# Hybrid decoder layer in fp32 on one core: the first FFN pass's norm and half of its operands made during the mixers, the sample states loaded ahead, an output projection placed later

## The chip, the core and the metric

The kernel runs on one core of a Trainium2 chip. Work is shared by TensorE (PE in the profile; PEld is its weight load), VectorE (DVE), ScalarE (ACT), GpSimd (POOL) and SyncE (SP), which here issues every DMA from one queue, in order. Each engine executes its own list of instructions in the order in which it was written. The metric is the time of one execution on the device in microseconds (us).

## The reference

One layer over 2048 prompt tokens and 8 x 4 sample tokens, width 1024. Two head groups run in parallel (the mixers): HGRN2, a gated linear recurrence with 4 heads, and a causal convolution of width 31 over 512 channels. Then comes a SwiGLU feed-forward network (FFN), a per-layer embedding behind a gate, and a last norm.

```python
xn = _rmsnorm(h, norm_mix)
proj = xn @ w_in                      # q, fg, iv, og, ca, cg
forget = lb + (1.0 - lb) * sigmoid(fg)
o, s_new = _hgrn2_scan(silu(q), 1.0 - forget, iv, log(forget), s0)
o_a = _rmsnorm(o, hgrn_out_norm) * silu(og)
u = ca * sigmoid(cg)
z = depthwise_conv(concat(buf0, u)) + conv_dw_bias
o_b = silu(layer_norm(z))
h = h + concat(o_a, o_b) @ w_out
xn2 = _rmsnorm(h, norm_ffn)
h = h + (silu(xn2 @ w_ffn_gate) * (xn2 @ w_ffn_up)) @ w_ffn_down
gate = sigmoid(_rmsnorm(h, norm_ple) @ w_ple_gate)
h = h + gate * (p_l @ w_ple_proj)
y = _rmsnorm(h, norm_final)
```

The sample tokens start from given states s0 (8 states of 128x128 for each head); the new states are outputs too.

## The kernel before

**Precision.** Every large product is made of three matmuls in fp32r: each operand is split into a high part (ACT copies it, tiles wh, xah, xoh, x2h) and a low part (DVE subtracts, tiles wl, xal, xol, x2l; `split` and `split_piece`, recorded at L368 and L373).

**Mixers.** The tokens are 8 blocks of 256 (the last has the 32 sample tokens as well), two blocks to a superblock, so superblocks 0 to 3. For each superblock PE makes 24 units of input projection (ca, cg, iv, f, q, og) from the normed operand XA and 8 units of output projection ("o") from XO. Superblocks 1 and 2 do both blocks in one matmul of 512 columns; 0 and 3 do them as two lanes of 256 (or 288) columns. The list `seq` sets the order of the units: after the units of superblock s, the first `AFTER` = 12 input units of s + 1, then the 8 output units of s, then the other input units of s + 1. Between them run the convolution (31 DVE taps for each channel group, L376), the recurrence (`hgrn`, 4 heads one after another for each block, one at a time) and, when all 4 channel groups of a block are there, the layer norm over channels (`layer_norm`, PE transposes L921 and L953). In the last block `hgrn` also takes the sample states: for each head 4 times it gets a tile of pool `tmp`, loads two states into it (t<-s_in), uses and updates them on PE (L1136, L1145) and DVE, and stores them. Pool `tmp` has 8 tiles, which the convolution and others use too.

**FFN.** When all that is recorded, the memory of the mixers is given over to the FFN's tiles (`open_scope("ffn")`), the event "ffn" is fired, and only then are the output units of superblock 3 recorded, on PE ahead of the FFN. The FFN goes over the tokens in 3 passes of two halves (348 tokens). Gate and up are a Strassen-like product with 7 combinations (A11, A12, S1, ...) of 4 quarter operands. For pass t `norm2(t)` loads the residual stream h1 back from DRAM, makes the row factors r2 of both halves (`rms2`: ACT squares, DVE sums, PE transposes L1618, DVE reductions L1613 to L1625, POOL power L409, PE transposes L1633), and `combine(t, kp, ...)` for kp = 0 to 3 loads and scales four pieces and splits the 7 combinations into slots X2. The slots of kp 0 and 1 lie in the memory of XA, those of kp 2 and 3 (x2h, x2l) in the FFN's memory. Pass 0 needs blocks 0 to 2 only.

The 22 hidden tiles go in chunks of 4, 4, 4, 4, 4, 2 (`CHUNKS`). After a chunk's gate and up (`gate_up`, L1354) comes the down product of the chunk before it (`down`), and at the end of a pass the down products of the last two chunks one after the other, then the gated embedding (`embed`). With the last down product each finished piece of h2 is split into an operand of the embedding (`h2_split`), which takes a slot of pool `hid` (16 slots; a hidden tile takes one for each half until its chunk's down product is done).

**Order.** A planner with fixed costs records each engine's instructions: of the steps that are ready it takes the one that could start first, and between steps of an engine that could start at nearly the same time the one with the lower number (the second argument of `spawn`; convolution 400 and 700, recurrence 0 and 250, weight splits 10, `combine` 0). Pools hand out buffers in the order of the requests.

Of the kernel before, what the change touches and what calls it, by code (L numbers as in the profile page):

```python
# [8 lines left out]
F32R = mybir.dt.float32r  # L9
# [23 lines left out]
CHUNKS = (4, 4, 4, 4, 4, 2)  # L33
# [22 lines left out]
AFTER = 12  # L56
# [179 lines left out]
def trunk(ctx: ExitStack, tc: tile.TileContext, x_in, p_in, s0_in, c0_in, w_in, w_out, w_gu, w_dn,  # L236
# [52 lines left out]


# [331 lines left out]
    def lane(L):  # L622
        for i, (s, u, lanes) in enumerate(seq):
# [362 lines left out]
    def hgrn(b, L, h, f):  # L986
# [130 lines left out]
        if samp:  # L1117
# [10 lines left out]
                     [scss, vs], [bo])  # L1128
            for g in range(4):
                s0 = yield acq(tmp)  # L1130
                s3 = s0.ap[:, 0:256].rearrange("p (b v) -> p b v", b=2)
                yield dma(s3, s0_in[h, :, 2 * g:2 * g + 2, :], W=[s0], nbytes=512 * 256)
# [16 lines left out]
                yield tt(s0.ap[:, 0:256], s0.ap[:, 0:256], b2.ap[:, 0:256], ALU.add, R=[s0, b2], W=[s0], n=256)  # L1149
# [3 lines left out]
                S.release(tmp, s0)  # L1153
# [41 lines left out]
        if done[b] == HEADS:  # L1195
            if samp:
                S.release(hg, *ivs.pop(b))
            S.fire(("hgdone", b))

# [17 lines left out]
    S.spawn(lane(1), 30)  # L1217
    manual = tc.manual_schedule()
# [8 lines left out]
    def cut(tiles, count):  # L1227

        return [tuple(Buf(t[:, i * WID:(i + 1) * WID]) for t in tiles) for i in range(count)]

    def flat(i, count):
        f = hbuf[i].rearrange("p k t -> p (k t)")
        return [Buf(f[:, j * WID:(j + 1) * WID]) for j in range(count)]

    xslots = cut(za, 16) + cut([tm("x2" + p, [128, 12 * WID], F32R) for p in "hl"], 12)
    X2 = [{name: xslots[kp * len(COMBOS) + i] for i, name in enumerate(COMBOS)} for kp in range(KP)]
# [7 lines left out]

    PASSES = range(len(HALF))
    HALVES = range(2)
    last_chunk = NCK - 1
# [304 lines left out]
    def segs(t, h):  # L1552

        lo, out = OFF[t] + h * HALF[t], []
        for b in range(NBLK):
            x, y = max(lo, b * BLK), min(lo + HALF[t], b * BLK + blk_n(b))
            if x < y:
                out.append((b, x - b * BLK, x - lo, y - x))
        return out

    def h1_load(t, h, k, q):
        n, lo = HALF[t], OFF[t] + h * HALF[t]
        for b, _, _, _ in segs(t, h):
            yield wait(("h1", b, k // 2))
        yield dma(q.ap[:, 0:n], h1d[:, k, lo:lo + n], W=[q], nbytes=512 * n)

    res, n3, pins = {}, {}, {}

    def residual():
        for t in PASSES:  # L1570
            for m in range(KD):
                for h in HALVES:
                    q = yield acq(hres)
                    yield from h1_load(t, h, m, q)
                    res[t, m, h] = q
                    S.fire(("hr", t, m, h))

    def free_h(b, idx, count):
        for i in range(KD // 2):
            yield wait(("h1", b, i))  # L1580
        S.release(hres, *flat(idx, count))

    def squares2(n, get, sq, tag):
        for k in range(KD):
            src, q = yield from get(k)
            yield act(q.ap[:, 0:n], src.ap[:, 0:n], AF.Square, scale=D ** -0.5, R=[src], W=[q], n=n)
            sq[k] = q
            S.fire(("sq", tag, k))

    def rms2(n, get):  # L1590

        tk = toks(n)
        tag, sq = count[0], {}
        count[0] += 1
        S.spawn(squares2(n, get, sq, tag), PSQ)
        acc = [None, None]
        for i in range(KD):
            yield wait(("sq", tag, i))
            if i < 2:
                acc[i] = sq[i]  # L1600
                continue
            a, q = acc[i % 2], sq[i]
            if i == 2:
                yield stt(a.ap[:, 0:n], a.ap[:, 0:n], EPS / 128, q.ap[:, 0:n], ALU.add, ALU.add, R=[a, q], W=[a], n=n)
            else:
                yield tt(a.ap[:, 0:n], a.ap[:, 0:n], q.ap[:, 0:n], ALU.add, R=[a, q], W=[a], n=n)
            S.release(tmp2, q)
        a, q = acc
        yield tt(a.ap[:, 0:n], a.ap[:, 0:n], q.ap[:, 0:n], ALU.add, R=[a, q], W=[a], n=n)
        S.release(tmp2, q)  # L1610
        ss = yield acq(small)
        tn = tk[-1][1]
        yield op("dve", 80.0, lambda: nc.vector.memset(ss.ap[:, 2:3], 1.0), [], [ss])  # L1613
        bank = yield acq(misc)

        def fn():
# [235 lines left out]
```

## Time and profile before

| | us |
|---|---|
| median of 3 runs | 2723.65 (2722.88 to 2724.57) |
| the profiled execution | 2725.04 |
| its span in the trace | 2723.3 |
| PE busy | 2566.1 (94%) |
| DVE busy | 1999.1 (73%) |
| ACT busy | 1071.4 (39%) |

The profiled execution took 1.7 us more than its span and lies 1.4 us over the median. PE carries nearly all of the span, so what can be read from the table is little; the question is where PE stood still or ran at a lower clock, and for what.

### The profile page before, as it was taken

How to read it: one execution, taken by the hardware profiler on the slowest of the kernel's cores; microseconds unless marked ns; L12 is line 12 of the kernel's file. 1: busy time of each engine (PE TensorE's matmuls, PEld its weight loads, DVE VectorE, ACT ScalarE, POOL GpSimd, SP SyncE). 2: the span in 40 equal slices, each digit the busy share in tenths (PEclk: the TensorE clock that was granted, in tenths of full speed). 3: DMA queues.
4: the chain of work that ended last, by engine and by line, in shares of the span. 5: the costliest groups of instructions: out<-in, count | busy, mean ns of one | idle time of the engine just before them, and what ended most of it. 6: DMA issues, size and time to landing. Idle time of an engine off the chain costs nothing.

```text
span 2723.3 us, 43381 instructions
## 1 busy us (share of the span) xinstructions
PE 2566.1 (94%) x15886; PEld 2409.8 (88%) x15886; DVE 1999.1 (73%) x4506; ACT 1071.4 (39%) x2397; POOL 134.1 (5%) x286
## 2 busy tenths in 40 slices
PE   7999899999998659999999899999998999999996
PEld 6988777778787559999999899999998999999996
DVE  8999888888768557666668686766677776666664
ACT  5553233333113225344444443544345444433441
POOL 0111011021001000000000000000000000000000
PEclk9999899999998679999999899999999999999998
DMA  8656555654555262232213133322232252212311
GB/s 307 219 189 220 179 173 197 207 171 147 183 175 168 94 196 74 71 116 78 82 62 111 66 118 115 123 78 71 70 113 65 81 158 82 75 66 77 101 47 50
DMA packets 219078, 338.66 MB, mean 124 GB/s; under 512 B 38640, under 2 KB 82160, under 8 KB 218864
## 3 DMA queue, kind: packets, MB, share of 16 engines
q1 hardware_dynamic: 218864, 335.89, 37.4%
q8 instruction: 124, 2.03, 0.3%
q14 instruction: 90, 0.74, 0.1%
HBM read 282.29 MB, written 53.51 MB: 123 GB/s over the span
## 4 chain that ended last, share of the span: by engine, by line
PE 89%; DVE 6%; DMA 2%; POOL 1%; ACT 1%; issue 1%; SPq 0%; DVEq 0%; POOLq 0%; ACTq 0%
PE pm L1354 20%; PE pm L525 14%; PE pm L527 13%; PE pm L526 13%; PE px L1354 12%; PE px L525 3%; PE px L527 3%; PE px L526 3%; DVE h L373 1%; PE pm L593 1%; PE pm L595 1%; PE pm L594 1%; DVE h L376 1%; DMA t<-s_in 1%; PE px L1113 1%; PE px L1080 1%
## 5 line engine op out<-in xcount | busy, mean ns | idle before, releaser
L373 DVE TENSOR_TENSOR wl<-raw,wh 128x512 fp32r<-128x512 f32 x520 | 356.4, 689 | 200.0 <-ACT wh L368 197.1
L368 ACT ACTIVATE wh<-raw 128x512 fp32r<-128x512 f32 x520 | 323.2, 627 | 380.7 <-PE pm L526 208.2
L527 PE MATMUL pm<-xoh,wl 128*128 128x348 f32 (+4 forms) x1072 | 350.0, 326 | 14.1 <-DVE wl L373 14.1
L525 PE MATMUL pm<-xol,wh 128*128 128x348 f32 (+4 forms) x1072 | 353.7, 330 | 1.9 <-DVE xol L373 1.6
L526 PE MATMUL pm<-xoh,wh 128*128 128x348 f32 (+4 forms) x1072 | 349.6, 326 | 0.0
L525 PE MATMUL pm<-xal,wh 128*128 128x256 f32 (+2 forms) x960 | 321.0, 334 | 5.9 <-DVE xal L373 3.5
L526 PE MATMUL pm<-xah,wh 128*128 128x256 f32 (+2 forms) x960 | 309.8, 323 | 0.0
L527 PE MATMUL pm<-xah,wl 128*128 128x256 f32 (+2 forms) x960 | 309.3, 322 | 0.0
L1354 PE MATMUL pm<-xal,wh 128*128 128x348 f32 (+1 forms) x661 | 213.6, 323 | 18.0 <-DVE xal L373 14.9
L373 DVE TENSOR_TENSOR h<-pm,h 128x348 f32<-128x348 f32 (+1 forms) x263 | 135.2, 516 | 122.9 <-PE pm L527 109.8
L527 PEld LDWEIGHTS pm<-xoh,wl 128*128 128x128 f32 x1072 | 205.5, 192 | 20.3 <-DVE wl L373 14.7
L368 ACT ACTIVATE wh<-tw 128x512 fp32r<-128x512 f32 x198 | 124.8, 630 | 244.2 <-DVE tw L373 120.5
L525 PEld LDWEIGHTS pm<-xol,wh 128*128 128x128 f32 x1072 | 205.7, 192 | 12.1 <-issue 3.8
L1354 PE MATMUL pm<-xah,wh 128*128 128x348 f32 (+1 forms) x661 | 212.6, 322 | 0.0
L1354 PE MATMUL pm<-xah,wl 128*128 128x348 f32 (+1 forms) x661 | 212.4, 321 | 0.0
L376 DVE SCALAR_TENSOR_TENSOR t<-u,cvw,t 128x256 f32<-128x256 f32 x448 | 212.1, 473 | 0.0
L526 PEld LDWEIGHTS pm<-xoh,wh 128*128 128x128 f32 x1072 | 205.5, 192 | 4.5
L525 PEld LDWEIGHTS pm<-xal,wh 128*128 128x128 f32 x960 | 182.1, 190 | 29.8 <-issue 6.5
L527 PEld LDWEIGHTS pm<-xah,wl 128*128 128x128 f32 x960 | 181.4, 189 | 13.9
L526 PEld LDWEIGHTS pm<-xah,wh 128*128 128x128 f32 x960 | 182.1, 190 | 12.1
L376 DVE SCALAR_TENSOR_TENSOR h<-u,cvw,h 128x256 f32<-128x256 f32 x360 | 170.3, 473 | 0.0
L409 POOL TENSOR_TENSOR sm<-sm,mhalf 128x2 f32<-128x2 f32 (+3 forms) x79 | 67.6, 855 | 1878.2 <-DVE sm L1613 824.3
(267 smaller groups left out, 6225.9 us busy)
## 6 DMA issues: line engine op xcount, KB each, us to landing
raw<-w_gu SPq DMA_DIRECT2D x264, 256.0 KB, 2.8
wh<-wch SPq DMA_DIRECT2D x192, 256.0 KB, 2.7
wl<-wcl SPq DMA_DIRECT2D x192, 256.0 KB, 3.1
raw<-w_dn SPq DMA_DIRECT2D x132, 256.0 KB, 2.8
wch<-wh SPq DMA_DIRECT2D x64, 256.0 KB, 2.6
wcl<-wl SPq DMA_DIRECT2D x64, 256.0 KB, 3.1
raw<-w_in SPq DMA_DIRECT2D x48, 256.0 KB, 3.8
raw<-w_pg SPq DMA_DIRECT2D x48, 256.0 KB, 2.8
```

Of the source, the lines that this page charges most:

```text
L368: nc.scalar.activation(out, in_, func, scale=scale, bias=bias, **kw)
L373: return op("dve", d_tt(n), lambda: nc.vector.tensor_tensor(out=out, in0=a, in1=b, op=o), R, W)
L376: return op("dve", d_tt(n, not isinstance(s, float)), lambda: nc.vector.scalar_tensor_tensor(out=out, in0=a, scalar=s, in1=b, op0=o0, op1= ...
L409: return op("pool", 700.0, lambda: nc.gpsimd.tensor_tensor(out=s.ap[0:rows, out:out + n], in0=s.ap[0:rows, lo:lo + n], in1=mhalf[0:rows, 0 ...
L525: nc.tensor.matmul(out, lhsT=wh, rhs=xl, start=first, stop=False)
L526: nc.tensor.matmul(out, lhsT=wh, rhs=xh, start=False, stop=False)
L527: nc.tensor.matmul(out, lhsT=wl, rhs=xh, start=False, stop=last)
L593: nc.tensor.matmul(bank.ap, lhsT=xs[0], rhs=wl, start=(k == 0), stop=False)
L594: nc.tensor.matmul(bank.ap, lhsT=xs[0], rhs=wh, start=False, stop=False)
L595: nc.tensor.matmul(bank.ap, lhsT=xs[1], rhs=wh, start=False, stop=(k == KD - 1))
L1080: nc.tensor.matmul(bu[e].ap[:, c], lhsT=kt.ap[p, c], rhs=V[i].ap[p, hc], start=True, stop=True)
L1354: nc.tensor.matmul(out, lhsT=a, rhs=b, start=first and i == 0, stop=last and i == 2, skip_group_check=True)
```

## The change

1. `AFTER` becomes (12, 12, 20, 0): the output units of superblock 2 come after 20 instead of 12 input units of superblock 3. The later superblocks take their input units in the order that superblock 0 had (ca and cg of the first group ahead of iv).
2. The sample states are loaded by a step of their own, `load_states`, two tiles of 128x512 of pool `raws` for a head (4 states each), from the end of superblock 2's input units on. Pool `raws` (6 tiles) holds weights during superblock 0 and in the FFN and is empty between.
3. `norm2(0)` and `combine(0, 0)`, `combine(0, 1)` are recorded with the mixers, with number 350, as soon as tiles are free: pool `tmp2` gets its 5 tiles in `hbuf[1]` when block 5's h1 is stored (`free_tmp2`), r2 gets memory of its own, and the combinations wait until superblock 3's input units are done with XA. kp 2 and 3 wait for "ffn".
4. `CHUNKS` becomes (4, 4, 4, 4, 2, 4), and `combine` of passes 1 and 2 gets number 150 instead of 0.

The functions `segs` to `combine` are moved ahead of the mixers' spawns with no other change than the lines shown.

```diff
-CHUNKS = (4, 4, 4, 4, 4, 2)
+CHUNKS = (4, 4, 4, 4, 2, 4)
...
-AFTER = 12
+AFTER = (12, 12, 20, 0)
...
+    r2 = [Buf(tl(f"r2{h}", [128, WID])) for h in range(2)]
...
+    tmp2 = S.pool("tmp2", [])
...
-        todo = list(in_units) if s + 1 < NSUP else []
-        add(s + 1, todo[:AFTER], then)
+        todo = list(first_units) if s + 1 < NSUP else []
+        add(s + 1, todo[:AFTER[s]], then)
         add(s, outs, who if s else AB)
-        add(s + 1, todo[AFTER:], then)
+        add(s + 1, todo[AFTER[s]:], then)
...
-                if u == in_units[-1]:
+                if u == first_units[-1]:
                     S.fire(("indone", b))
...
+            yield wait(("s0", h))
+            two = stash.pop(("s0", h))
             for g in range(4):
-                s0 = yield acq(tmp)
-                s3 = s0.ap[:, 0:256].rearrange("p (b v) -> p b v", b=2)
-                yield dma(s3, s0_in[h, :, 2 * g:2 * g + 2, :], W=[s0], nbytes=512 * 256)
+                s0 = two[g // 2]
+                sa = s0.ap[:, g % 2 * 256:g % 2 * 256 + 256]
+                s3 = sa.rearrange("p (b v) -> p b v", b=2)
...
-                S.release(tmp, s0)
+            S.release(raws, *two)
...
+    def load_states():
+        yield wait(("indone", NBLK - 4))
+        for h in range(HEADS):
+            two = yield acq(raws, 2)
+            for g, s0 in enumerate(two):
+                yield dma(s0.ap.rearrange("p (b v) -> p b v", b=4), s0_in[h, :, 4 * g:4 * g + 4, :], W=[s0],
+                          nbytes=512 * 512)
+            stash["s0", h] = two
+            S.fire(("s0", h))
+
+    def free_tmp2():
+        for i in range(KD // 2):
+            yield wait(("h1", NBLK - 3, i))
+        S.release(tmp2, *flat(1, 5))
...
+    xslots = cut(za, 16)
+    X2 = [{name: xslots[kp * len(COMBOS) + i] for i, name in enumerate(COMBOS)} for kp in range(2)]
...
     def norm2(t):
...
         if t:
             yield wait(("a", t - 1, last_chunk, CHUNKS[-1] - 1, 1))
+        else:
+            yield wait(("indone", NBLK - 2))
+            yield wait(("indone", NBLK - 1))
         for kp in range(KP):
+            if t == 0 and kp == 2:
+                yield wait("ffn")
             five = yield acq(tmp2, 5)
-            S.spawn(combine(t, kp, five), 0)
+            S.spawn(combine(t, kp, five), 350 if t == 0 and kp < 2 else 150 if t else 0)
...
+    S.spawn(load_states(), 0)
+    S.spawn(free_tmp2(), 0)
+    S.spawn(norm2(0), 350)
...
-    tmp2 = S.pool("tmp2", [Buf(tm(f"f{i}", [128, WID])) for i in range(NTMP2)] + flat(1, 5))
+    S.release(tmp2, *[Buf(tm(f"f{i}", [128, WID])) for i in range(NTMP2)])
-    r2 = [Buf(tm(f"r2{h}", [128, WID])) for h in range(2)]
...
     for t in PASSES:
-        S.spawn(norm2(t), 100 if t else 0)
+        if t:
+            S.spawn(norm2(t), 100)
```

Three places show how the instructions move. **PE, from the last output unit of superblock 3 to the first gate product of the FFN** (px and pm are PSUM banks, f and h here tiles of the norm, sm its row sums; L1354 is the FFN's matmul). Before:

```order
L527 MATMUL px_177<-xoh,wl_91 128x288
L1618 MATMUL px_178<-idn,f_9007 128x128 x2
L1618 MATMUL px_178<-idn,f_9007 92x128
L1633 MATMUL px_176<-idn,sm_68 128x128 x2
L1633 MATMUL px_176<-idn,sm_68 128x92
L1618 MATMUL px_178<-idn,h_77 128x128 x2
L1618 MATMUL px_178<-idn,h_77 92x128
L1633 MATMUL px_176<-idn,sm_70 128x128 x2
L1633 MATMUL px_176<-idn,sm_70 128x92
L1354 MATMUL pm_173<-xal,wh_92 128x348
```

Of the change (L537 is the old L527, L1528 the old L1354):

```order
L535 MATMUL pm_174<-xol,wh_90 128x288
L536 MATMUL pm_174<-xoh,wh_90 128x288
L537 MATMUL pm_174<-xoh,wl_91 128x288
L1528 MATMUL pm_175<-xal,wh_92 128x348
L1528 MATMUL pm_175<-xah,wh_92 128x348
```

The four transposes of `norm2(0)` no longer stand between the output units and the FFN.

**PE, from the last input unit of superblock 3 to its first output unit** of the change (L1148 and L1157 are the sample states' matmuls, the old L1136 and L1145; L931 and L963 the layer norm's transposes; L1304 and L1319 those of `norm2(0)`):

```order
L537 MATMUL pm_173<-xah,wl_95 128x288
L1148 MATMUL px_180<-raw_103,t_152 32x128 x2
L1319 MATMUL px_178<-idn,sm_74 128x128 x2
L1319 MATMUL px_178<-idn,sm_74 128x92
L1157 MATMUL px_177<-t_155,t_148 128x256
L1148 MATMUL px_180<-raw_103,t_152 32x128 x2
L1157 MATMUL px_177<-t_154,t_148 128x256
L1194 MATMUL px_179<-idn,t_153 128x128 x2
L1196 MATMUL px_179<-idn,t_151 128x32
L1304 MATMUL px_178<-idn,h_77 128x128 x2
L1304 MATMUL px_178<-idn,h_77 92x128
L931 MATMUL px_177<-idn,h_78 128x128 x4
```

Before, six of the sixteen sample-state steps and the whole recurrence of two heads stood here; now two steps do, and one head's last transposes.

**DVE, the end of the last down product of pass 0** (h<-pm,h adds a down result to the residual, xol<-h,gn,xoh is `h2_split`, x2l and xal are combinations for pass 1). Before:

```order
L373 TENSOR_TENSOR h_78<-pm_174,h_78 128x348
L373 TENSOR_TENSOR h_78<-px_177,h_78 128x348
L373 TENSOR_TENSOR x2l<-f_9011,x2h 128x348
L376 SCALAR_TENSOR_TENSOR xol<-h_78,gn,xoh 128x348 x2
L373 TENSOR_TENSOR x2l<-f_9008,x2h 128x348
```

Of the change:

```order
L383 TENSOR_TENSOR h_78<-pm_174,h_78 128x348
L386 SCALAR_TENSOR_TENSOR xol<-h_79,gn,xoh 128x348
L386 SCALAR_TENSOR_TENSOR xol<-h_78,gn,xoh 128x348 x3
L386 SCALAR_TENSOR_TENSOR xol<-h_79,gn,xoh 128x348
L386 SCALAR_TENSOR_TENSOR xol<-h_78,gn,xoh 128x348 x3
L383 TENSOR_TENSOR wl_87<-raw_100,wh_86 128x512
L383 TENSOR_TENSOR xal<-f_9123,xah 128x348
```

Eight of the sixteen operand splits now follow the last add, and most combinations for pass 1 follow those.

## Rows read from the trace of the kernel before

**Rows 1.** The page: busy time of engines, and the span in 40 slices.

```profile
PE 2566.1 (94%) x15886; PEld 2409.8 (88%) x15886; DVE 1999.1 (73%) x4506; ACT 1071.4 (39%) x2397; POOL 134.1 (5%) x286
...
PE   7999899999998659999999899999998999999996
...
PEclk9999899999998679999999899999999999999998
```

**Rows 2.** Windows, mixers to FFN: length; busy (count) of each engine; PEclk, DMA share, GB/s.

```profile
core 0: us, PE busy (x) PEld busy (x) DVE busy (x) ACT busy (x) POOL busy (x), PEclk, DMA share, GB/s
100.00:300.00 200.00, 188.91 (x1293) 164.85 (x1292) 185.99 (x502) 87.29 (x252) 26.54 (x64) 0.98 0.55 186
633.00:867.50 234.50, 232.20 (x1538) 201.51 (x1537) 175.96 (x526) 55.25 (x163) 22.87 (x61) 1.00 0.56 174
633.00:922.30 289.30, 261.43 (x1638) 217.66 (x1636) 218.39 (x683) 65.63 (x201) 27.47 (x76) 0.91 0.49 154
750.00:800.00 50.00, 49.50 (x347) 44.45 (x346) 27.48 (x82) 9.14 (x27) 3.62 (x13) 1.00 0.58 180
867.50:934.10 66.60, 36.21 (x129) 20.55 (x127) 49.05 (x172) 13.52 (x47) 8.12 (x23) 0.55 0.18 59
934.10:985.50 51.40, 50.63 (x385) 50.40 (x384) 17.07 (x35) 9.41 (x20) 0.00 (x0) 0.96 0.71 236
985.50:1025.00 39.50, 6.90 (x22) 4.20 (x22) 29.18 (x66) 15.94 (x35) 1.71 (x2) 0.56 0.51 156
1025.00:1050.00 25.00, 24.57 (x135) 24.08 (x136) 18.87 (x37) 13.66 (x29) 0.00 (x0) 0.88 0.16 53
```

**Rows 3.** Waits of PE, 860 to 1030 us: us in total, times, longest.

```profile
PE px L1136 <- DMA t<-s_in: 22.4, 6, 4.4
PE pm L1354 <- DVE xal L373: 14.9, 3, 8.6
PE px L1618 <- DVE sm L1613: 11.7, 2, 7.6
```

**Rows 4.** Timeline of PE, the last layer norm: start, length, idle before and releaser.

```profile
922.27 2.82 PE L921 MATMUL px<-idn,h 128*128 128x128 f32 x12
...
934.05 0.58 PE L525 MATMUL pm<-xol,wh 128*128 128x256 f32 x1
```

**Rows 5.** Windows of the three ends of pass, columns as in group 2.

```profile
1490.00:1500.00 10.00, 5.88 (x34) 5.05 (x32) 10.00 (x23) 5.81 (x13) 0.00 (x0) 0.92 0.25 71
1500.00:1510.00 10.00, 3.62 (x11) 3.18 (x12) 10.00 (x22) 7.39 (x17) 0.00 (x0) 0.50 0.22 68
1510.00:1520.00 10.00, 8.41 (x48) 7.88 (x46) 9.12 (x24) 6.37 (x15) 0.97 (x1) 0.90 0.29 90
1520.00:1530.00 10.00, 9.50 (x59) 9.09 (x60) 4.94 (x11) 3.43 (x7) 1.76 (x2) 1.00 0.09 28
2050.00:2060.00 10.00, 9.12 (x57) 8.63 (x56) 10.00 (x23) 5.93 (x13) 0.00 (x0) 1.00 0.03 8
2060.00:2070.00 10.00, 1.80 (x10) 1.25 (x9) 10.00 (x23) 6.22 (x14) 0.00 (x0) 0.75 0.22 64
2070.00:2080.00 10.00, 9.32 (x45) 9.32 (x46) 10.00 (x24) 7.81 (x19) 0.00 (x0) 0.74 0.33 105
2080.00:2090.00 10.00, 8.27 (x56) 7.94 (x55) 5.39 (x16) 2.76 (x8) 3.01 (x1) 1.00 0.08 29
2600.00:2620.00 20.00, 14.62 (x92) 14.33 (x91) 19.40 (x44) 14.62 (x33) 0.00 (x0) 0.95 0.04 14
2620.00:2640.00 20.00, 20.00 (x118) 19.86 (x118) 10.46 (x25) 6.36 (x13) 2.00 (x2) 0.88 0.24 79
```

**Rows 6.** Timeline of DVE in the first of them.

```profile
1499.29 0.51 DVE L373 TENSOR_TENSOR h<-pm,h 128x348 f32<-128x348 f32 x1
1499.72 0.51 DVE L373 TENSOR_TENSOR h<-px,h 128x348 f32<-128x348 f32 x1
1500.15 0.51 DVE L373 TENSOR_TENSOR x2l<-f,x2h 128x348 fp32r<-128x348 f32 x1
1500.58 1.06 DVE L376 SCALAR_TENSOR_TENSOR xol<-h,gn,xoh 128x348 fp32r<-128x348 f32 x2
1501.56 0.51 DVE L373 TENSOR_TENSOR x2l<-h,x2h 128x348 fp32r<-128x348 f32 x1
...
1508.66 1.28 DVE L373 TENSOR_TENSOR wl<-raw,wh 128x512 fp32r<-128x512 f32 x2
1509.86 0.51 DVE L376 SCALAR_TENSOR_TENSOR f<-f,h 128x348 f32<-128x348 f32 x1
```

**Rows 7.** Timeline of PE there: down matmuls at full clock, then the longest wait.

```profile
1495.35 0.32 PE L525 MATMUL px<-xol,wh 128*128 128x348 f32 x1
1495.51 0.33 PE L526 MATMUL px<-xoh,wh 128*128 128x348 f32 x1
...
1506.31 0.66 PE L525 MATMUL pm<-hxl,wh 128*128 128x348 f32 x1 [10.32 <-ACT wh L368]
```

**Rows 8.** Waits of the SP queue, 850 to 1030 us, and one weight load, 860 to 935.

```profile
SPq L454 <- DVE h L373: 22.1, 9, 5.6
...
wl<-wcl SPq DMA_DIRECT2D x5, 256.0 KB, 5.7
```

More of the change, by code (lines that the diff above doesn't have):

```diff
@@ L288, in trunk, with flat @@
     wcache = [dram.tile([64, 128, 512], F32, name="wc" + p) for p in "hl"]
+    r2 = [Buf(tl(f"r2{h}", [128, WID])) for h in range(2)]
+    def flat(i, count):
+        f = hbuf[i].rearrange("p k t -> p (k t)")
+        return [Buf(f[:, j * WID:(j + 1) * WID]) for j in range(count)]
+    tmp2 = S.pool("tmp2", [])
     open_scope("mix")
@@ new lines, in cut, with segs @@
+    def cut(tiles, count):
+        return [tuple(Buf(t[:, i * WID:(i + 1) * WID]) for t in tiles) for i in range(count)]
+    PASSES = range(len(HALF))
+    HALVES = range(2)
+    last_chunk = NCK - 1
+    xslots = cut(za, 16)
+    X2 = [{name: xslots[kp * len(COMBOS) + i] for i, name in enumerate(COMBOS)} for kp in range(2)]
+    def segs(t, h):
+        lo, out = OFF[t] + h * HALF[t], []
+        for b in range(NBLK):
+            x, y = max(lo, b * BLK), min(lo + HALF[t], b * BLK + blk_n(b))
+            if x < y:
+                out.append((b, x - b * BLK, x - lo, y - x))
+        return out
@@ new lines, in h1_load, with residual @@
+    def h1_load(t, h, k, q):
+        n, lo = HALF[t], OFF[t] + h * HALF[t]
+        for b, _, _, _ in segs(t, h):
+            yield wait(("h1", b, k // 2))
+        yield dma(q.ap[:, 0:n], h1d[:, k, lo:lo + n], W=[q], nbytes=512 * n)
+    res, n3, pins = {}, {}, {}
+    def residual():
+        for t in PASSES:
+            for m in range(KD):
+                for h in HALVES:
+                    q = yield acq(hres)
+                    yield from h1_load(t, h, m, q)
+                    res[t, m, h] = q
+                    S.fire(("hr", t, m, h))
@@ new lines, in row, with norm2, get @@
+    def row(n, get, r, ev):
+        bank = yield from rms2(n, get)
+        yield act(r.ap[:, 0:n], bank.ap[:, 0:n], AF.Copy, R=[bank], W=[r], n=n)
+        S.release(misc, bank)
+        S.fire(ev)
+    def norm2(t):
+        if t:
+            yield wait(("a", t - 1, 2, 0, 1))
+        for h in HALVES:
+            def get(k, h=h):
+                q = yield acq(tmp2)
+                yield from h1_load(t, h, k, q)
+                return q, q
+            yield from row(HALF[t], get, r2[h], ("r2", t, h))
+        if t:
+            yield wait(("a", t - 1, last_chunk, CHUNKS[-1] - 1, 1))
+        else:
+            yield wait(("indone", NBLK - 2))
+            yield wait(("indone", NBLK - 1))
+        for kp in range(KP):
+            if t == 0 and kp == 2:
+                yield wait("ffn")
+            five = yield acq(tmp2, 5)
+            S.spawn(combine(t, kp, five), 350 if t == 0 and kp < 2 else 150 if t else 0)
@@ L1567, in trunk @@
[L1567 to L1588, printed above, removed]
@@ L1639, in row @@
-    def row(n, get, r, ev):
-        bank = yield from rms2(n, get)
-        yield act(r.ap[:, 0:n], bank.ap[:, 0:n], AF.Copy, R=[bank], W=[r], n=n)
-        S.release(misc, bank)
-        S.fire(ev)
-    def norm2(t):
-        if t:
-            yield wait(("a", t - 1, 2, 0, 1))
-        for h in HALVES:
-            def get(k, h=h):
-                q = yield acq(tmp2)
-                yield from h1_load(t, h, k, q)
-                return q, q
-            yield from row(HALF[t], get, r2[h], ("r2", t, h))
-        if t:
-            yield wait(("a", t - 1, last_chunk, CHUNKS[-1] - 1, 1))
-        for kp in range(KP):
-            five = yield acq(tmp2, 5)
-            S.spawn(combine(t, kp, five), 0)
```

176 lines of the change are left out of this document (83 added, 93 removed).

## The prediction

> **What bounds the kernel now.** First the page: PE is busy 94% of the span, DVE 73%, and in the 40 slices PE dips at the mixers' end (8, 6, 5) and slightly at three later places; the granted clock dips in the same slices [rows 1]. So the kernel is bound by PE except there, and a change can only gain where PE stands still or runs at the lower of its two clock levels (1.2 instead of 2.4 GHz, a granted clock of 0.50). I therefore cut the dips into windows.
>
> At the end of the mixers [rows 2] PE is full until 867.5 us, when superblock 3's input units end. From 867.5 to 934.1 it is busy 36.21 of 66.6 us at a granted clock of 0.55: these are the small matmuls of the recurrence, waiting for DVE, ACT and, for 22.4 us in six pieces, for the sample states' loads [rows 3]. From 934.1 to 985.5 it makes the output units, full. From 985.5 to 1025 it is busy 6.90 of 39.5 us at 0.56: `norm2(0)` and the first combinations, DVE work on which PE waits (L1618 11.7 us, xal 14.9 us) [rows 3]. At 1025 the gate product runs for good.
>
> Behind that, each pass has a hole at the last down product [rows 5]. There DVE is busy 10.00 of 10 us, and PE waits 10.32 us for a weight whose split is queued behind other work [rows 6, 7]. The output projection's and FFN's other stretches are full, and nothing is to be had there.
>
> **The change part by part.** The sum is made against the profiled execution's 2725.04 us, 1.4 us over the median 2723.65; the difference goes through unchanged.
>
> *Mixers to FFN (parts 1 to 3).* What PE does from 867.5 to 1025 is, counted at full clock, 36.21 x 0.55 + 50.63 x 0.96 + 6.90 x 0.56 = 19.9 + 48.6 + 3.9 = 72.4 us of 157.5 [rows 2]. With every wait gone the gate product could start at 867.5 + 72.4 = 939.9, 85.1 us sooner, and the 24.57 us behind 1025 at 0.88 would save another 2.9: a ceiling of 88.0 us. The parts share it and can't be added singly: state loads alone are in it with at most 22.4.
>
> Can DVE follow? The operands of superblock 3 are split at 633, and from there to the layer norm of the last block (922.3) DVE is busy 218.4 of 289.3 us, 75% [rows 2]. Its idle 71 us lie mostly before 867.5 (234.5 - 176.0 = 58.5), the worst stretch being 750 to 800 at 55%, when PE works on the output units of superblock 2 and hands DVE little. Those units now come 8 input units later, so DVE gets superblock 3's convolutions and heads earlier. To its 218.4 us the change adds the sums of `norm2(0)`: 14 adds, 0.43 us apart [rows 6], and four reductions of about 0.35, 7.4 us together. So 226 us; at the 93% that DVE reaches from 100 to 300 [rows 2] that is 243 us, and the layer norm can start at 876. PE has 867.5 plus what it no longer does in the tail: of the 19.9 us some 16 now lie among the projections, so it arrives at about 884. PE is the later one, by 8 us.
>
> From the layer norm to the first output unit took 11.8 us (922.27 to 934.05) [rows 4], about 3.4 us of it PE work at full clock (6.8 at half), so 8.4 are kept. The output units kept 0.96 of the clock; I keep their 2.0 us too. I give 2 to 3 more for DVE being late here and there. That leaves 85.1 + 2.9 - 8.4 - 2.0 - 2.6 = **75 us**.
>
> The moved work must be hidden: a combination group is 4 scalings 0.49 us apart (1.06 for two in [rows 6]) and 11 adds or splits of 0.43, 6.7 us of DVE, four groups 26.8. Two are written ahead of the output units and two beside them. Beside the 51.4 us of output units DVE was busy only 17.07 [rows 2]; there now fall 13.4 us of kp 2 and 3, perhaps 13 of kp 0 and 1 if late, 16 adds of about 0.4 (6.4) and 11 weight splits or differences of 0.60 (6.6): 39 of 51.4. If that cover were gone, the old stall of 39.5 us would be back.
>
> Loads: the states are 8 loads of 256 KB instead of 16 of 128 KB, issued around 633, before superblock 3's first head has its operands, and hidden there; the fourth head's tiles come from the first's. The 32 loads of h1 for `norm2(0)` and `combine(0)` move on the SP queue ahead of weights of superblock 3's output units. SP already stands waiting for DVE to free tiles (22.1 us in nine waits) [rows 8]. A wait there holds the weights behind it, but four of the eight output units have theirs loaded before, 25 us of PE work. The Trainium skill, "DMA: Bandwidth & Descriptors", Anatomy of one DMA, says that a DMA's semaphore wait is taken on the issuing sequencer before dispatch, so everything behind it on that queue is late too; by that rule the moved loads could give back part of the gain, which is a rival below. The rows on SP agree that the queue waits, but show no PE wait on wch or wcl in that stretch.
>
> The new order of units at a superblock's start (ca and cg before iv): superblock 3's ca needs all 8 operand pieces in 2.6 us of PE where iv took longer, so PE may wait a little for splits; against it convolutions start earlier. Between 0 and +3 us per superblock; I take 0 and leave 5 in the range.
>
> *Ends of pass (part 4).* The holes [rows 5], idle time plus busy time x (1 - granted clock): pass 0, 4.1 + 6.4 + 1.6 + 0.5 idle and 3.1 of clock, 15.7; pass 1, 0.9 + 8.2 + 0.7 + 1.7 and 2.9, 14.4; pass 2, 5.4 and 3.1, 8.5. Together 38.6 us. Cause: with a last chunk of 2, PE takes 6 matmuls of 0.16 us [rows 7] for a piece of h2, 0.96 us, and DVE owes for each an add 0.43, an operand split 0.49, a sum for the norm 0.43 and weights 0.15: 1.5 us. With a chunk of 4 PE takes 1.92, DVE 1.65, and combinations, which had come ahead of weight splits, now come after. The chunk of 2 stands one down product earlier, where DVE owes only the add and weights, 0.6 against 0.96.
>
> What it costs: the last chunk now holds 8 of the 16 slots of `hid` until its last matmul, so eight operand splits fall behind it. The embedding uses the first four k of half 0 in 1.9 us, then wants one each 0.48 us while a pair of splits takes about 1: 1 to 2 us of waiting a pass. PE's waits for the norm's transposes stay (about 1.8 in passes 0 and 1). Kept: 9 of 38.6, gain **30 us** (ends: 0, if the late splits cost what the hole did, and 38.6).
>
> Sum: 75 + 30 = 105; 2725.04 - 105 = 2620, and for the median 2723.65 - 105 = **2619 us**.
>
> **The rivals.**
>
> *DVE keeps its pace of 75%* because it is held by chains of small steps and not by lack of work. Then 226 us take 301, the layer norm starts at 934, the output units at 946, the gate product at 997: 28 + 3 us gained, with the 30 of the passes 2663. For it: head after head runs one at a time. Against it: 93% in the first superblocks. The halfway house is 2641.
>
> *The end of pass stays*, moved from the weights to the late operand splits: 75 + 0 to 10, 2639 to 2649. For it: DVE and ACT are both loaded there, and splits of weights and pins fall in the same place. Against it: the order shows the first weights of the embedding ahead of the eight splits.
>
> *The SP queue*: the loads of kp 1 wait for kp 0 to be done, and the last four output units' weights stand behind. One combination group late plus one landing of 5.7 us [rows 8] is about 12 to 15 us: 2632. This is the page's rule at work.
>
> *Slower.* Twenty input units in a row ask DVE for more than it gives; ca banks stay held for convolution buffers and PE starves where before it had output units to do. Price: if all of 633 to the layer norm ran at the 55% of 750 to 800, 226 us would take 411, the layer norm would start at 1044 and the gate product at 1107, 82 us later than now; less the 30 of the passes that is 2776. It decides from a DVE share below about 63% (layer norm after 992), where 75% was measured.
>
> *That the change does nothing* is excluded for the transition by the order of PE: no transposes stand before the first gate product.
>
> **How the numbers follow.** Likeliest, 2600 to 2640: 0.70, with 2619 its middle. DVE at its old pace, 2640 to 2670: 0.12. End of pass stays: 0.10. SP: 0.04. Slower or no change: 0.04. The floor is 2723.65 - 88.0 - 38.6 = 2597. The range goes from 2599, near the floor, to 2655, which leaves out half of the DVE case, the slower case and little else. Faster by over 0.2% (5.4 us, what a measurement of this kernel can tell): 0.95; within it 0.02; slower 0.03.
>
> **What the changed profile would show.** Right: no PE wait on s_in; DVE over 85% from 633 to the layer norm, which begins near 885; output units from about 897; gate product for good near 950, without transposes L1304 or L1319 just before it; no PE wait over 3 us at the ends of pass, and the granted clock 1.00 there. Wrong: PE idle between 633 and 870, waiting for DVE or ACT in superblock 3; output units waiting for wh or wl from DMA; the first gate products waiting for x2l; or a wait at the embedding's start for xol or hxl of 5 us or more. The forecast fails if DVE's idle time there is latency that no reordering fills.

## The result, and the profile after

The changed kernel takes 2676.78 us (2673.62 to 2679.3, 4 runs) where the kernel before took 2724.11 beside it: a ratio of 0.9825, 95% interval 0.9808 to 0.9842. That is 47 us faster, where 105 were forecast and 2599 to 2655 was the range. The profiled execution took 2673.62, its span 2671.9, 51.4 less than before. The page of after, engines and slices (against [rows 1]):

```profile
PE 2552.0 (96%) x15886; PEld 2402.9 (90%) x15886; DVE 2003.0 (75%) x4506; ACT 1076.4 (40%) x2397; POOL 142.6 (5%) x286
...
PE   7999899999999699999998999999998999999996
...
PEclk9999999999999799999999999999998999999998
```

One deep dip is left at the mixers' end, and small ones at the ends of passes 0 and 1 (slices 22 and 31). The transition in windows, cut at the last input unit of superblock 3, the last layer norm, the first output unit, and the first gate product for good (columns as in [rows 2]):

```profile
635.00:888.50 253.50, 248.80 (x1607) 210.68 (x1606) 209.26 (x642) 68.77 (x204) 31.43 (x74) 0.99 0.57 171
888.50:906.25 17.75, 5.47 (x24) 3.07 (x23) 17.08 (x64) 7.10 (x21) 3.19 (x5) 0.64 0.55 165
906.25:920.87 14.62, 7.09 (x28) 4.70 (x27) 10.49 (x23) 3.14 (x7) 4.12 (x7) 0.50 0.15 43
920.87:977.33 56.46, 52.02 (x385) 51.58 (x385) 37.30 (x79) 18.01 (x39) 0.00 (x0) 0.94 0.70 233
977.33:1002.00 24.67, 24.67 (x158) 24.67 (x157) 18.63 (x33) 12.45 (x24) 0.00 (x0) 1.00 0.44 136
...
635.00:906.25 271.25, 254.27 (x1629) 213.75 (x1628) 226.34 (x705) 75.87 (x225) 34.62 (x79) 0.97 0.57 171
750.00:800.00 50.00, 50.00 (x328) 41.60 (x328) 41.18 (x137) 15.65 (x49) 10.51 (x23) 1.00 0.45 134
```

The operands of superblock 3 are split at 635 (633 before), and the gate product runs for good from 977.33 instead of 1025. PE is full to 888.5; then it stands while DVE is busy 17.08 of 17.75 us. From 635 to the layer norm DVE is busy 226.34 of 271.25, 83.4%. The gate product no longer waits: 24.67 of 24.67 us at 1.00, where [rows 2] had 24.57 of 25 at 0.88. What PE waited for there (in total, times, longest):

```profile
PE px L1194 <- ACT t L378: 4.9, 1, 4.9
PE px L963 <- DVE h L394: 4.8, 2, 2.9
PE pm L535 <- DVE h L383: 4.2, 1, 4.2
PE px L1304 <- DVE sm L1299: 3.0, 1, 3.0
```

The waits for s_in and xal of [rows 3] are gone; the one for the norm's row is 3.0 us instead of 11.7 and stands ahead of the layer norm. The ends of pass, against [rows 5]:

```profile
1450.00:1460.00 10.00, 4.58 (x29) 4.29 (x27) 7.36 (x16) 4.32 (x9) 0.00 (x0) 0.84 0.49 137
1460.00:1470.00 10.00, 6.89 (x32) 6.90 (x33) 8.58 (x20) 6.70 (x15) 0.00 (x0) 0.65 0.10 33
1470.00:1480.00 10.00, 5.90 (x33) 4.56 (x31) 7.35 (x19) 3.92 (x10) 1.92 (x2) 0.87 0.16 52
1480.00:1490.00 10.00, 9.73 (x50) 9.60 (x50) 5.50 (x12) 4.41 (x11) 0.00 (x0) 0.79 0.08 26
2020.00:2030.00 10.00, 1.79 (x8) 1.50 (x7) 6.92 (x16) 4.45 (x10) 0.00 (x0) 0.67 0.47 141
2030.00:2040.00 10.00, 9.24 (x48) 8.96 (x46) 7.90 (x19) 6.84 (x16) 0.00 (x0) 0.82 0.03 6
2040.00:2050.00 10.00, 6.41 (x24) 5.22 (x25) 8.26 (x22) 3.60 (x10) 1.92 (x2) 0.70 0.15 48
...
2570.00:2590.00 20.00, 19.46 (x128) 19.11 (x127) 13.08 (x30) 9.12 (x19) 3.13 (x2) 1.00 0.17 52
```

By the prediction's measure (idle time plus busy time x (1 - granted clock)) pass 0 now loses 12.9 + 6.0 = 18.9 us and pass 1 12.6 + 4.2 = 16.7, where they lost 15.7 and 14.4; only pass 2, which has no combinations beside it, is cured (0.5, was 8.5). The timelines of PE and DVE at the wait of pass 0:

```profile
1454.26 0.32 PE L537 MATMUL pm<-wh,wl 128*128 128x348 f32 x1
1463.11 0.66 PE L535 MATMUL pm<-wl,wh 128*128 128x348 f32 x1 [8.53 <-DVE wl L383]
```

```profile
1446.09 4.02 DVE L386 SCALAR_TENSOR_TENSOR xol<-h,gn,xoh 128x348 fp32r<-128x348 f32 x8
...
1459.80 0.58 DVE L386 SCALAR_TENSOR_TENSOR f<-f,gn,r 128x348 f32<-128x348 f32 x1 [0.93 <-DMA f<-h1d]
1461.55 0.58 DVE L386 SCALAR_TENSOR_TENSOR h<-h,gn,r 128x348 f32<-128x348 f32 x1 [1.17 <-DMA h<-h1d]
1462.05 0.57 DVE L386 SCALAR_TENSOR_TENSOR f<-f,gn,r 128x348 f32<-128x348 f32 x1
1462.54 0.51 DVE L383 TENSOR_TENSOR wl<-f,wh 128x348 fp32r<-128x348 f32 x1
...
1476.70 0.06 DVE L1299 MEMSET sm<- 128x1 f32 x1
```

The eight late operand splits were over at 1450.1 and nobody waited for them over 1 us. PE waits for a `wl` that is not a weight: it is the low part of the embedding's fourth input piece (`pin_load`: a tile of `tmp2`, a load of p_in, a split into a slot of the weights' ring), and it comes behind the scalings of a combination group. The memset at 1476.70 stands at the end of the second norm row's sums, late as well.

Bookkeeping of the 51.4 us of span: the gate product runs for good 47.7 us sooner (1025 to 977.33, with superblock 3's start 2 later in it), and from there to the end it is 1694.6 instead of 1698.3 us, of which 3 are the clock behind the first gate product. So the transition, with that clock as in the forecast, gave about 50 and the ends of pass 1 to 3 (their holes went from 38.6 to 36.1).

These stages are those of one execution, the fastest of the four. Seven of the experiments below (e2, e5, e6, e9, e12, e13, e14) have the same instructions up to the first gate product and reach it at 979.5 to 985.6. From the split of superblock 3's operands, which ends there at 634.8 to 638.9, to the layer norm they take 272 to 277 us, with DVE 81.7 to 83.2% busy. e1, which has the mixers of before, has its gate product for good from 1031.3 instead of 1025. A stage of a single profile is therefore known to some 6 to 8 us.

### The profile page after: what moved, and what is told of

It reads as the page before. It is cut to its first block, busy times and chain, and to the rows that moved or that the text cites. A ratio compares the mean times of both kernels' runs of the same rounds, so it can differ in the third digit from the quotient of the medians.

```text
span 2671.9 us, 43353 instructions
## 1 busy us (share of the span) xinstructions
PE 2552.0 (96%) x15886; PEld 2402.9 (90%) x15886; DVE 2003.0 (75%) x4506; ACT 1076.4 (40%) x2397; POOL 142.6 (5%) x286
## 4 chain that ended last, share of the span: by engine, by line
PE 66%; DVE 3%; DMA 1%; ACT 1%; POOL 0%; issue 0%; SPq 0%; DVEq 0%; POOLq 0%; ACTq 0%
PE pm L1528 23%; PE px L1528 10%; PE pm L535 8%; PE pm L536 7%; PE pm L537 7%; PE px L537 3%; PE px L535 3%; PE px L536 3%; DMA h<-h1d 1%; DVE h L383 1%; DVE h L386 1%; POOL sm L419 0%; DVE xol L386 0%; PE px L1319 0%; PE px L1157 0%
## 5 line engine op out<-in xcount | busy, mean ns | idle before, releaser
L537 PE MATMUL pm<-xoh,wl 128*128 128x348 f32 (+4 forms) x1062 | 345.9, 326 | 0.2 <-DVE wl L383 0.2
L537 PE MATMUL pm<-xah,wl 128*128 128x256 f32 (+2 forms) x960 | 310.2, 323 | 0.5 <-DMA wl<-wcl 0.5
L1528 PE MATMUL pm<-xal,wh 128*128 128x348 f32 (+1 forms) x725 | 234.0, 323 | 8.3 <-DVE h L383 4.3
L1528 PE MATMUL pm<-xah,wh 128*128 128x348 f32 (+1 forms) x725 | 232.6, 321 | 0.0
L1528 PE MATMUL pm<-xah,wl 128*128 128x348 f32 (+1 forms) x725 | 232.5, 321 | 0.0
L537 PEld LDWEIGHTS pm<-xoh,wl 128*128 128x128 f32 x1062 | 203.1, 191 | 6.3 <-DVE wl L383 0.4
L537 PEld LDWEIGHTS pm<-xah,wl 128*128 128x128 f32 x960 | 181.8, 189 | 14.9 <-DMA wl<-wcl 1.1
L1528 PE MATMUL pm<-x2h,wh 128*128 128x348 f32 (+1 forms) x547 | 176.1, 322 | 0.0
L1528 PE MATMUL pm<-x2h,wl 128*128 128x348 f32 (+1 forms) x547 | 175.8, 321 | 0.0
```

The lines of the kernel that those rows point to most:

```text
L537: nc.tensor.matmul(out, lhsT=wl, rhs=xh, start=False, stop=last)
L1528: nc.tensor.matmul(out, lhsT=a, rhs=b, start=first and i == 0, stop=last and i == 2, skip_group_check=True)
```

## The experiments

Each time stands with its ratio to the kernel before on the same chip (2726.9 to 2729.5 us); the intervals are 0.001 to 0.002 on either side. Against the changed kernel ratios are compared with 0.9825, and 0.001 is 2.7 us; two kernels are told apart from some 6 us on.

**Ends of pass: is part 4 worth anything?** Part 4 alone in the kernel before (e1), and the changed kernel without it (e6).

```diff
-CHUNKS = (4, 4, 4, 4, 4, 2)
+CHUNKS = (4, 4, 4, 4, 2, 4)
-            S.spawn(combine(t, kp, five), 0)
+            S.spawn(combine(t, kp, five), 150 if t else 0)
```

e1: 

> The kernel before with part 4 alone (chunks 4, 4, 4, 4, 2, 4 and number 150 for the combinations of passes 1 and 2). Theory 'pins': the hole of pass 2, which has no combinations beside it, goes (8.5 us), while in passes 0 and 1 the hole only moves from the weights to the embedding's fourth input piece, which stands behind combinations: about 4 us faster than before, 2716 to 2721. Rival 'the two parts meet badly': part 4 by itself gives the 30 us of the prediction, about 2694, and only together with parts 1 to 3 loses them.

e6: 

> The changed kernel with part 4 undone (chunks 4, 4, 4, 4, 4, 2; combinations of passes 1 and 2 with number 0). Prediction's term: 30 us slower. After e1, where part 4 alone gave nothing: within 6 us of the changed kernel, 2674 to 2686, the first gate product at 977 as before, and the old holes at the ends of the passes in place of the new ones.

e1 measured 2729.09 us, 1.0001 (0.9991 to 1.001); e6 2681.29, 0.9815 (0.9794 to 0.9836). Part 4 gives nothing that could be told, by itself or with the rest. e1 shows the same two waits for the piece (16.7 us, longest 8.4), e6 the old ones for weights (10.3, 8.7, 5.4).

**What do the combinations cost?** e12 leaves them out for passes 1 and 2.

```diff
+            if t:
+                for name in COMBOS:
+                    S.fire(("x2", t, kp, name))
+                continue
             five = yield acq(tmp2, 5)
```

> The changed kernel without the combinations of passes 1 and 2 (their loads, scalings, sums and splits left out; the gate and up products of these passes read pass 0's operands, so TensorE does the same work). This bounds what they cost. Theory 'combinations in the way': no wait of TensorE over 3 us at the end of any pass, 25 to 35 us faster than the changed kernel, 2642 to 2656. Rival 'late operand splits' (the eight that part 4 puts behind the last add): waits of 5 us or more for operands (xol or hxl) stay at the embedding's start of each pass, 2662 or later.

2641.86 us, 0.9678 (0.9658 to 0.9697): some 39 us under the changed kernel. From the first gate product to the end no wait of PE is over 2.5 us. The late operand splits, which are still there, cost nothing; the combinations cost all of it.

**Holding them back.** Three kernels hold the combinations of passes 1 and 2 ever longer: e2 until the pieces are split, e5 until the row factors r3 are there too, e9 until the second column of the embedding is done.

```diff
             yield wait(("a", t - 1, last_chunk, CHUNKS[-1] - 1, 1))
+            for k in range(2):
+                for h in HALVES:
+                    yield wait(("pin", t - 1, k, h))
+            for h in HALVES:
+                yield wait(("r3", t - 1, h))
```

These are e5's lines; e2 has the first three of them, and e9 in their place a wait for ("h3", t - 1, 1, h).

e2: 

> The changed kernel, with the combinations of passes 1 and 2 held until the four input pieces (pins) of the pass before are loaded and split. Theory 'pins': the waits of 8.5 and 8.2 us at the start of the embedding of passes 0 and 1 go, and with them some 6 us of lower clock: 20 to 24 us faster than the changed kernel, 2653 to 2657. Rival 'DVE is overloaded there': the debt is only handed on, to the eight late operand splits or to the first gate product of the next pass, and the time stays within 5 us of the changed kernel's 2677.

e5: 

> As e2, and the combinations of passes 1 and 2 wait for the row factors r3 of the pass before as well. In e2 the input pieces came early, but the ten tiles of tmp2 went to two combination groups ahead of the squares of the second norm row, and TensorE, whose order has that row's transposes ahead of the embedding's third product, stood 24.6 and 23.1 us for them. Theory 'what the embedding's start needs stands behind combinations in tmp2': now neither pieces nor rows do, no wait of TensorE over 2 us at the ends of passes 0 and 1: 18 to 25 us faster than the changed kernel, 2653 to 2662 (e2 minus 40). Rival 'DVE has too much to do there': the combinations, 27 us of DVE, don't fit beside the rest of the embedding, and the next pass's first gate product waits: 2670 or later.

e9: 

> The changed kernel, with the combinations of passes 1 and 2 held until the second of the embedding's eight output columns of the pass before is finished (all that the embedding's start needs has then had the tiles of tmp2 and DVE to itself). Theory 'combinations in the way': the ends of passes 0 and 1 become like that of pass 2, which has none; waits of TensorE there under 3 us each, 10 us sooner than e5, about 2658. Rival 'DVE has too much to do': the 27 us of combinations come too late for the next pass's first gate product, which waits 5 us or more, or the embedding's banks come free late all the same; within 4 us of e5's 2669.

e2: 2700.45 us, 0.9896 (0.9879 to 0.9912), slower by 19. The wait for the piece is gone, but the waits of PE from the first gate product on are headed by another:

```profile
PE px L1304 <- DVE sm L1299: 50.3, 3, 24.6
```

These are the transposes of the second norm row, which PE's order has ahead of the embedding's next product. e5: 2669.36, 0.9787 (0.9772 to 0.9801), 10 faster; PE still waits 4.8, 6.2 and 3.8 us for ACT; at 1476.77 it is the tanh that empties a gate's PSUM bank, which ended at 1476.72. e9: 2700.01, 0.9890 (0.9876 to 0.9905): x2l comes 7.8 us late for each next pass. Each theory had part of it: what the embedding needs does stand behind the combinations, but held back for long they come too late themselves.

**Tiles or time?** e13 asks for the five tiles of the next group only when the group before is done; e14 does the same with the waits of e5.

```diff
         for kp in range(KP):
+            if t and kp:
+                yield wait(("x2", t, kp - 1, "S3"))
             five = yield acq(tmp2, 5)
```

e13: 

> The changed kernel with the combination groups of passes 1 and 2 one after another: the next asks for its five tiles of tmp2 only when the one before is done, so that a group never holds all ten tiles and a request for five seldom stands ahead of others. Theory 'tiles': what hurts at the ends of passes is that pieces, squares and gate evacuations wait for tiles of tmp2 behind two groups; 15 us or more faster than the changed kernel, 2662 or sooner. Rival 'DVE's time': it is the 27 us of DVE work itself, in whatever order; within 6 us of the changed kernel, 2672 to 2684.

e14: 

> e13 with the wait of e5 (groups one after another, and only after the pieces and row factors of the pass before). Theory 'tiles': the waits of e5 for gate banks (4.8, 6.2 and 3.8 us) go too: 2655 to 2662. Rival 'DVE's time': e5's time, 2666 to 2672, or later, with the next pass's first gate product waiting for x2l as in e9.

e13: 2643.47 us, 0.9688 (0.9669 to 0.9708), some 37 faster than the changed kernel and 85 faster than before: within the intervals of e12, where that work is left out altogether. Windows and rows of DVE's timeline of e13:

```profile
1450.00:1460.00 10.00, 9.47 (x60) 8.97 (x58) 9.53 (x24) 6.57 (x14) 1.39 (x1) 1.00 0.14 48
1460.00:1470.00 10.00, 8.29 (x55) 8.16 (x55) 7.47 (x18) 3.81 (x9) 2.74 (x2) 1.00 0.43 126
1470.00:1480.00 10.00, 10.00 (x65) 10.00 (x64) 8.99 (x20) 6.06 (x14) 0.00 (x0) 1.00 0.24 79
```

```profile
1441.41 0.51 DVE L383 TENSOR_TENSOR wl<-f,wh 128x348 fp32r<-128x348 f32 x1
...
1459.94 0.06 DVE L1299 MEMSET sm<- 128x1 f32 x1
```

The last split of a piece stands at 1441.41 instead of 1462.54, the second row's memset at 1459.94 instead of 1476.70, with the same DVE work in the kernel. That it was the tiles is seen at the piece itself. In the changed kernel the two loads of the fourth piece left after PE had begun to stand (1454.6), the first of them when a combination's sum had let go of its tile (SP's timeline, and SP's wait between 1438 and 1465):

```profile
1456.94 0.33 SPq L464 DMA_DIRECT2D f<-p_in  x1
1457.79 0.42 SPq L464 DMA_DIRECT2D f<-p_in  x1
SPq L464 <- DVE f L383: 1.7, 1, 1.7
```

In e13 the last of these loads left at 1434.27. `tmp2` has ten tiles; two groups hold all of them, and since the pool serves requests in order, a request for five stops the requests for one behind it. Only the last 2 us of the piece's wait, from its high part at 1460.6 to the split at 1462.54, are DVE's order. For the squares of the second row tiles and DVE's time are not separated, since e13 also moves two groups behind this stretch (their first x2l is written at 1477.90 instead of 1452.13).

e14: 2722.22, 0.9979 (0.9970 to 0.9988): groups that are late and one at a time leave the gate product of passes 1 and 2 waiting 22.3 and 27.4 us for x2l. That is for the most part not DVE's time, as the rival had it: of these waits DVE itself stood idle 12.9 and 20.5 us for the groups' loads of h1, which the SP queue has behind the stores of the pass's output y. In pass 1, SP and then DVE:

```profile
1539.51 5.65 SPq L464 DMA_DIRECT2D y<-h  x12
1557.56 0.45 SPq L464 DMA_DIRECT2D f<-h1d  x1
1560.14 0.58 DVE L386 SCALAR_TENSOR_TENSOR f<-f,gn,r 128x348 f32<-128x348 f32 x1 [12.86 <-DMA f<-h1d]
```

No run has e13's wait without part 4, so what part 4 gives beside it is not shown, save for the 8 us of pass 2.

**The transition: what does each part give?** e7 puts superblock 2's output units back to 12 (the first edit), e3 keeps the norm of pass 0 back (the second), e8 is the kernel before with the state loads alone (its edit is part 2 of the change).

```diff
-AFTER = (12, 12, 20, 0)
+AFTER = (12, 12, 12, 0)
...
         if t:
             yield wait(("a", t - 1, 2, 0, 1))
+        else:
+            yield wait("ffn")
```

e7: 

> The changed kernel with the output units of superblock 2 put back after 12 of superblock 3's input units (only that number of part 1 undone). Prediction's step 'DVE gets superblock 3's work sooner by the later output units': without it DVE's share from 750 to 800 falls back toward 55%, the last layer norm starts 10 to 20 us later (915 to 925) and the kernel is 10 to 20 us slower, 2686 to 2697. Rival 'the order of the output units is worth nothing, since DVE catches up while TensorE makes them': layer norm at 902 to 912, time within 5 us of 2677.

e3: 

> The changed kernel with the norm and combinations of pass 0 kept back until superblock 3's output units are recorded (part 3 undone, parts 1, 2 and 4 kept). Theory 'loads of h1': the moved norm's loads, which stand in SP's queue behind weights, hold ACT and DVE, which execute in order; without them the last layer norm starts at 890 us or sooner (906 in the changed kernel). Rival 'chains': DVE is paced by the recurrence's small steps, and only the work of the sums goes: layer norm at 896 or later. By both the norm's chain stands again ahead of the first gate product, so the whole kernel is slower, 2690 to 2710.

e8: 

> The kernel before with part 2 alone: the sample states loaded ahead in two tiles a head. If the 22.4 us in which TensorE waited for these loads lay on the path, the layer norm starts some 20 us sooner (about 902) and the kernel is about 20 us faster than before, 2704 to 2709. Rival 'the loads lay beside DVE's work' (DVE was 75% busy there): DVE's next steps end the wait instead, and at most 8 us are gained, 2717 or later.

e7: 2710.33 us, 0.9933 (0.9917 to 0.9950), 29 slower. e3: 2702.99, 0.9908 (0.9888 to 0.9928), 23 slower. e8: 2718.95, 0.9970 (0.9960 to 0.9981), 8 faster than before. Windows of e7 (up to the bulk of the layer norm's transposes) and of e3 (to its layer norm), then a wait of e8:

```profile
750.00:800.00 50.00, 49.14 (x323) 44.50 (x322) 22.45 (x65) 10.53 (x26) 2.82 (x11) 1.00 0.70 220
635.00:950.73 315.73, 267.82 (x1650) 222.28 (x1648) 237.47 (x711) 83.08 (x245) 35.65 (x80) 0.89 0.51 153
```

```profile
635.00:897.50 262.50, 253.58 (x1642) 213.50 (x1640) 218.73 (x678) 70.17 (x214) 34.21 (x78) 0.99 0.56 168
```

```profile
PE px L921 <- DVE h L373: 14.7, 2, 11.4
```

With the units at 12 DVE falls to 45% from 750 to 800 and to 75% on the whole, the pace of before: their place carries most of the gain. In e3 superblock 3's operands are split at 637.5 (634.9 in the changed kernel). Counted from there, DVE has 216.3 us to do instead of 226.4, the layer norm comes after 260.0 us instead of 271.3, and DVE's share is 83.2%, as with the norm: the moved work costs its own time, and no more than that can be told. With the states loaded ahead, PE waits for the convolution's sums on DVE instead: of 22.4 us of waiting 8 were worth something.

**The SP queue.** e4 issues the first pass's loads of h1 from GpSimd (and the planner reckons them as DMAs); e16 is e5 with that.

```diff
-        yield dma(q.ap[:, 0:n], h1d[:, k, lo:lo + n], W=[q], nbytes=512 * n)
+        out, src = q.ap[:, 0:n], h1d[:, k, lo:lo + n]
+        if t:
+            yield dma(out, src, W=[q], nbytes=512 * n)
+        else:
+            yield op("pool", 60.0, lambda: nc.gpsimd.dma_start(out=out, in_=src), (), [q], 512 * n)
```

e4: 

> The changed kernel with the loads of h1 for pass 0 (norm and combinations, and its residual pieces) issued by GpSimd instead of SyncE, so that they stand behind nothing on SP's queue and SP's weights behind none of them. Theory 'loads of h1': the layer norm at 890 to 900, no wait of DVE for h1d over 1 us in the mixers, no wait of 4 us by an output unit for the residual's add; gate product for good 8 to 15 us sooner, 2662 to 2669. Rival 'chains': the layer norm stays at 902 to 908 and the time within 5 us of 2677.

e16: 

> e5 with the loads of h1 for pass 0 issued by GpSimd as in e4. If the two gains (about 10 us and 4 us) lie in separate stretches they add: 2664 to 2667 where e5 gave 2669. Rival: e4's small difference was chance; 2667 to 2672.

e4: 2676.40 us, 0.9810 (0.9795 to 0.9824), not told apart from 0.9825; its layer norm starts at 901.3, but PE then waits 7.9 us for a residual's add. e16: 2669.69, 0.9789, e5's time. Counted from superblock 3's operands the layer norm does come sooner (after 266 us in both, 271 to 277 with the loads on SP), but PE's longer wait for the residual (8.6 us in e16) gives it back. These loads' place on the queue costs the kernel a few us at most; what the queue can cost elsewhere, e14 showed.

**Can DVE's idle time be filled?** e15 plans with another latency; e17 (the second edit) and e18 are e13 with the output units after 24 and 16 input units.

```diff
-    LAT = 200.0
+    LAT = 400.0
...
-AFTER = (12, 12, 20, 0)
+AFTER = (12, 12, 24, 0)
```

e15: 

> The changed kernel with the planner's latency between engines at 400 ns instead of 200, so that it puts independent work (convolution taps) between the dependent steps of the recurrence. For DVE from the operands of superblock 3 to the last layer norm, 83.5% busy in the changed kernel. Theory 'order': the idle time there is that of a queue in order behind steps that come later than planned, and can be filled: 88% or more, layer norm at 899 or sooner. Rival 'chains': no filling work is there at those times; 80 to 86%, layer norm at 902 or later. The rest of the kernel is ordered anew as well, so the time is not compared.

e17: 

> e13 with the output units of superblock 2 after all 24 of superblock 3's input units instead of 20. Theory 'TensorE hands DVE its work too late' (12 to 20 gave about 30 us): another step in the same direction, DVE over 85% busy to the last layer norm, which starts at 902 or sooner, and 2 to 8 us gained on e13, 2636 to 2642. Rival 'given back': the residual of superblock 2 is stored later, so the moved norm's loads and tiles come later and fall on the layer norm and the output units; e13's time or up to 15 us more.

e18: 

> e13 with those output units after 16 input units. Theory 'TensorE hands DVE its work too late': between e7's and the changed kernel's transition, the layer norm 5 to 15 us later than 906 and 8 to 18 us lost on e13, 2652 to 2662. Rival: the step from 12 to 20 is made in its first half already, and 16 costs nothing, 2640 to 2648.

e15: 2692.61 us; DVE to the end of the layer norm's transposes:

```profile
635.00:921.91 286.91, 252.01 (x1604) 210.38 (x1602) 230.54 (x713) 78.13 (x231) 43.61 (x80) 0.93 0.55 161
```

80.4% (its operands are split at 624, its first transpose stands at 906.4), so theory 'order' fell, at least by this lever. e17: 2653.81, 0.9726 (0.9710 to 0.9742), 10 slower than e13: the layer norm's first transpose stands at 897.3, but its last at 910.7, DVE is 81% busy up to there, and PE waits 8.8 us for the moved norm's sums and 8.8 for a residual's add. e18: 2655.17, 0.9731 (0.9717 to 0.9746), 12 slower, its layer norm held 18.9 us by taps. 20 is the best of the four places tried (12 without e13's wait).

One run combines: e10 is e9 with the moved norm behind the taps.

```diff
-    S.spawn(norm2(0), 350)
+    S.spawn(norm2(0), 800)
```

> As e9, and the norm and first two combinations of pass 0 have number 800 instead of 350, behind the last block's convolution taps (700), on which the last layer norm waits. Theory 'backlog': DVE has some 8 us less in front of the layer norm, which starts near 898 as in e3, and the first gate product comes up to 8 us sooner than 977. Rival 'given back': the norm's chain, now later, ends behind the output units or collides with the layer norm's own chain; the gate product at 977 or later. Time from e9 minus 8 to e9 plus 15.

2704.16 us, 0.9905 (0.9890 to 0.9920), e9's time. The layer norm started at 902.3, but an output unit then waited 11.4 us for a residual's add: given back.

## Why the prediction was wrong, point by point

**Ends of pass: forecast 30, measured 1 to 3. The step that failed is the cause.** I set DVE's debt of 1.5 us against PE's 0.96 for each piece of h2, took the wait for a late weight split as its sign, and put the combinations at nothing once they came after the weight splits. The remedy shifted that debt, and in pass 2, where nothing else competes, it did work. In passes 0 and 1 a second debtor stood behind the first: combination groups that hold all tiles of `tmp2`, some 39 us by e12. In pass 0 the wait went from a weight's `wh` (10.32 us in [rows 7]) to a piece's `wl` (8.53 us), at the same place. My rival 'the end of pass stays' had the place and most of the size, but blamed the eight late operand splits; e12 acquits them. I had counted time on DVE and not who holds tiles, though the pools' order stood in the description.

**Transition: forecast 75, measured about 50. The mechanism was right, the term of DVE's pace was mis-sized.** DVE's work was 226 us as forecast (226.34), PE was done at 888.5 (forecast 884), but DVE's share was 83.4%, not the 93% that I took from 100 to 300. So the layer norm came at 906.25 and not at 885: 21 of the 27 us by which the gate product missed the forecast's 'near 950'. The other 6: layer norm to output units took 14.6 us (12 forecast), and the output units 56.5 (53), with one wait of 4.2 us for a residual's add. The rival that DVE keeps its 75% holds with the units at 12 (e7), so the step 'the later output units hand DVE its work sooner' is shown, and worth some 29 us. The sum of shares held too: the states alone give 8, not 22.4.

**The rest.** The new order of units cost 2 us up to superblock 3's start in this profile and up to 6 in the seven others, within the 0 to 3 for each superblock. The SP queue did wait: a residual's load stood 17.1 us there for the layer norm's split, with loads of h1 behind it. The Trainium skill, "DMA: Bandwidth & Descriptors", Anatomy of one DMA, says that a DMA's semaphore wait is taken on the issuing sequencer; the trace agrees. e4 and e16 show that little hangs on it in the transition. 'Slower' and 'no change' did not come.

**What stays open.** Why DVE reaches 83% there. The list of DVE's waits from 635 to 906 in the changed kernel begins so:

```profile
DVE raw L383 <- PE px L1157: 7.8, 6, 2.0
DVE scst L1075 <- PE px L1068: 6.4, 4, 4.7
DVE h L383 <- PE pm L537: 5.2, 6, 1.2
DVE tst L383 <- PE px L1090: 3.5, 4, 1.0
```

Many waits of 1 to 2 us for results of PE, most of them steps of the recurrence. That these are the chain's own latency is read, not shown: e15 tried one way of filling them, and no run took the recurrence apart.

## What to carry to other kernels

When a wait at a seam names a late step, ask not only what its engine does but which buffers it needed, and who held them: a request for several buffers at the head of a pool that serves in order stops everything behind it, and one wait that makes it ask later was worth as much as leaving the work out. Asking too late cost more than that (e14), since the loads then stood behind stores on the one queue. When two causes stand behind one wait, curing the first moves the wait without shortening it; the stretch that lacks the second (here pass 2) tells them apart before anything is run. A busy share taken from another stage is a hope: take it from a stretch with the same chain of steps, or bound it by both.

## What the runs showed of the hardware

Short stalls cost clock here beyond their own length. In the changed kernel PE stood for 8.53 us from 1454.6 to 1463.1 and was idle for another 4.1 between 1470 and 1480; the granted clock was 0.65, 0.87 and 0.79 in the windows from 1460 to 1490 (1.00 is 2.4 GHz, 0.50 is 1.2, the means lie between). That is 5.2 us lost beside the 12.9 us idle from 1450 to 1490. In e13, whose longest two gaps there are 1.7 and 0.5 us, the clock stayed at 1.00.
